# FoX scores with a full-height low pass, and mLSTM and sample FoX prepared one step ahead, in a hybrid decoder layer

## The chip, the cores and the metric

One Trainium2 chip, one of its cores. The metric is the device time of one execution in microseconds (us), lower is better. The kernel before takes 2261.63 us (median of 3 runs, 2254.97 to 2266.15).

## What is computed

One layer of a hybrid decoder for a prompt of 1024 tokens and a sample group of 8 sequences x 4 new tokens (32 rows), width 1024. One input projection `h @ w_in` feeds three mixers; their outputs are gated, merged and projected; cross attention and an MLP follow. All of it is float32. Of the mixers three matter here:

```python
# FoX: forgetting attention, 8 heads x 64, causal
s = einsum('bqhd,bkhd->bhqk', q, k) * hd**-0.5 + F_q - F_k      # F = cumsum(log sigmoid(f))
p = softmax(where(pos_q >= pos_k, s, -inf)); y = p @ v
# sample group: the same over 512 cached positions, gathered by page, and 4 new ones

# mLSTM: matrix memory, 4 heads x 128, chunk by chunk with a carried state C, n, m
d_w = exp(log_d - m_t); inter_w = exp(log_inter - m_t)
s   = (q @ k.T) * d_w
num = s @ v + inter_w * (C @ q); den = sum(s) + inter_w * (n . q)
h   = num / max(|den|, exp(-m_t))
C, n = a_end * C + (w_end * k).T @ v, a_end * n + (w_end * k) summed
y   = rmsnorm(h) * sigmoid(mo)
```

The prompt's mLSTM runs in 8 chunks of 128 tokens. The sample group's mLSTM is one chunk of 32 rows with 8 states that are loaded and written back.

## The kernel before

A float32 product is formed from float32r halves, in three passes: high x high, high x low, low x high (`mm3`, `split`). `load_u` and `load_tm` load 512 KB of weights from SP's queue (L61) into `wraw` (2 buffers); ScalarE writes the high half (`uh`, L54) and VectorE the low half (`ul`, L55). The products go into PSUM tiles called `mm`. The mixers use PSUM tiles `aux` (3) and `big` (1, two banks, for the scores).

The work is written as generators, and `weave` decides which of two takes the next step: the one that has got less far, by planned TensorE us (`k.pe`, counted from the matmuls' columns and from amounts added by hand) over a planned total. The line that matters:

```python
weave(k, (chain(pr["mq"], stage_gates(k)), 302.0), (mixers(), 312.0, 0.045, 0.95))
```

The main stream here is the projection of `mq` and of the gates, 28 weight units of 3 x 8 x 3 matmuls of 128 rows and 384 or 288 columns. The mixers run beside it from 4.5% to 95% of its way, in the order of `mixers()`: GLU, FoX of the prompt (`stage_fox`), mLSTM of the sample group (`stage_ml_sample`), then mLSTM of the prompt (`stage_ml`) together with FoX of the sample group (`stage_fox_sample`), woven by `beside` (so many steps of the first for one of the second), then the loading of two finished branches (`load_y`).

The order of writing is a priority, not yet the order on an engine: the framework's planner sorts each engine's instructions by a modelled time, taking the first in priority whose inputs are ready by its model. So gate matmuls stand between the four transposes of one mixer step in the trace. On the chip each engine and each DMA queue then follows this fixed order, and waits where the model was wrong.

Buffers: each stage has a pool of SBUF that is released at its end; the next stage's pool takes the same memory and must wait for the last reads of what lay there, DMA reads too. Within a pool a name has one to six buffers in turn.

`stage_fox` takes two heads at a time, at partitions 0 to 63 and 64 to 127. `KK[j]` has head j's keys as the high half on its own 64 partitions and the low half on the other 64. `QH[j]` has the query's high half on both, so one pass of 128 rows gives high x high and high x low. `QL` has the low halves of both heads, each on its own partitions; the second pass uses 64 rows of `QL` and of `KK[j]` (L229 is the helper that issues every matmul, L233 every transpose). A bf16 product with `identb` adds the causal mask. Widths go from 128 to 1024 columns, in pieces of up to 512, over 8 query blocks.

`ml_chunk` does one mLSTM chunk: it loads `km`, `v1`, `og` from POOL's queue (L1199), sets the ones column of `v1` on POOL (L1202), loads the row vector `E` broadcast to all partitions from SP's queue (L1204), adds the mask on VectorE (L1205) and takes the exponential on ScalarE (L1207); it transposes `km` into `kT`. Then come scores (`q,kT`), their product with `E` (L1217), `kw` (L1220), `num` from `v,E` and `CT,q`, the normalisation (L1231 to L1245), the state update (`v,kw`), and the tail: transposes of `yml` and the write to `S_yb`. `delayed_tails` takes the tail of one chunk after the second step of the next. Everything of a chunk is written in that chunk.

`stage_fox_sample` gathers pages of 128 positions x 512 values with indirect DMAs from POOL (L1067 keys, L1100 values) into `kt` (6 buffers), four for each of 16 steps, in the step that uses them. Its matmuls use one quarter of the array's columns per sequence (`tile_position`).

Of the kernel before, what the change touches and what calls it, by code (L numbers as in the profile page):

```python
# [18 lines left out]
P = 128  # L19
# [875 lines left out]
def stage_fox(k):  # L895
    nc, A, S = k.nc, k.A, k.S
    V, T, Sc = nc.vector, k.T, nc.scalar
    with ExitStack() as es:
        pool = es.enter_context(k.tc.tile_pool(name="fox", bufs=1, reuse_waits="tile"))
        for hp in range(4):  # L900
            cs = slice(hp * P, hp * P + P)

            KK = [pool.tile([P, NP], F32R, name="KK%d" % j) for j in range(2)]
            QH = [pool.tile([P, NP], F32R, name="QH%d" % j) for j in range(2)]
            QL = pool.tile([P, NP], F32R, name="QL")
            v = pool.tile([P, 8, P], F32, name="v", bufs=2)
# [10 lines left out]
            for i, tm in enumerate(tms):  # L917
                for h in range(2):
                    pt = k.aux.tile([P, 512], F32, name="aux")
                    for a in range(4):  # L920
                        T.transpose(pt[:, a * P:a * P + P], tm[:, 4 * h + a], k.ident)
                    c = slice(512 * h, 512 * h + 512)
                    for j in range(2):
                        r, o = half[j], half[1 - j]
                        hi = (KK, QH)[i][j]
                        Sc.activation(hi[r, c], pt[r], AF.Copy)
                        if i == 0:
                            V.tensor_tensor(hi[o, c], pt[r], hi[r, c].bitcast(F32), op=OP.subtract)
                        else:
                            Sc.activation(hi[o, c], pt[r], AF.Copy)  # L930
                            V.tensor_tensor(QL[r, c], pt[r], hi[r, c].bitcast(F32), op=OP.subtract)
                    k.pe += 1.5
                    yield
# [3 lines left out]
            def scores(u):  # L937
                qt, j = units[u]
                nk = (qt + 1) * P
                rows = slice(64 * j, 64 * j + 64)  # L940
                ps = k.big.tile([P, 1024], F32, name="big")
                for c0 in range(0, nk, 512):
                    n = min(512, nk - c0)
                    qc = slice(qt * P, qt * P + P)
                    T.matmul(ps[:, c0:c0 + n], QH[j][:, qc], KK[j][:, c0:c0 + n], start=True, stop=False)
                    T.matmul(ps[:, c0:c0 + n], QL[rows, qc], KK[j][rows, c0:c0 + n], start=False, stop=c0 + n < nk)
                T.matmul(ps[:, nk - P:nk], k.identb, k.maskq, start=False, stop=True)
                s = pool.tile([P, NP], F32, name="s", bufs=2)[:, :nk]
                mx = pool.tile([P, 1], F32, name="mx", bufs=2)
                V.tensor_tensor_reduce(s, ps[:, :nk], nF[j][:, :nk], 1.0, -3.0e38, OP.add, OP.max, mx)  # L950
                nm = pool.tile([P, 1], F32, name="nm", bufs=2)
                V.tensor_scalar(nm, mx, -1.0, None, op0=OP.mult)
# [79 lines left out]
def stage_fox_sample(k, pool):  # L1032
# [14 lines left out]
    for j in range(2):  # L1047
        r = slice(64 * j, 64 * j + 64)
        for b in range(4):
            dst = Qb[r, :, b].rearrange("p s (t h) -> p s t h", h=8)[:, :, :, 2 * b + j]  # L1050
            V.tensor_copy(dst, pq[r, b * NS:b * NS + NS].rearrange("p (s t) -> p s t", t=4))
    for g in range(2):
        pS = k.aux.tile([P, 512], F32, name="aux")
# [8 lines left out]
        for j in range(4):  # L1062
            kts = []
            for i in range(4):
                s = 4 * g + i
                kts.append(pool.tile([P, 512], F32, name="kt", bufs=6))
                nc.gpsimd.indirect_dma_start(  # L1067
                    out=kts[i], out_offset=None, in_=A["kp"],
                    in_offset=bass.IndirectOffsetOnAxis(ap=k.idx[:, 4 * s + j:4 * s + j + 1], axis=0))
# [25 lines left out]
        for j in range(4):  # L1095
            vts = []
            for i in range(4):
                s = 4 * g + i
                vts.append(pool.tile([P, 512], F32, name="kt", bufs=6))
                nc.gpsimd.indirect_dma_start(  # L1100
                    out=vts[i], out_offset=None, in_=A["vp"],
                    in_offset=bass.IndirectOffsetOnAxis(ap=k.idx[:, 4 * s + j:4 * s + j + 1], axis=0))
# [5 lines left out]
        Y = pool.tile([P, 512], F32, name="kt", bufs=6)  # L1108
        V.tensor_tensor(Y, pO, k.maskh, op=OP.mult)
# [78 lines left out]

def ml_chunk(k, pool, ti, n, qf, mask, inter, state):

    nc, S = k.nc, k.S
    V, T, Sc = nc.vector, k.T, nc.scalar
    t0 = TT[ti][0]
    km = pool.tile([P, 4, P], F32, name="km", bufs=2)[:n]
    v1 = pool.tile([P, 4, 129], F32, name="v1", bufs=2)[:n]
    og = pool.tile([P, 4, P], F32, name="og", bufs=2)[:n]
    for t, nme in ((km, "mk"), (v1, "mv"), (og, "og")):
        if ti < 8:
            nc.gpsimd.dma_start(t[:, :, 0:P], S[nme][t0:t0 + n, :].rearrange("p (a b) -> p a b", a=4))  # L1199
        else:  # L1200
            load_s(k, t, nme)
    nc.gpsimd.memset(v1[:, :, P:129], 1.0)  # L1202
    E = pool.tile([P, 4, P], F32, name="E", bufs=2)[:n, :, :n]
# [8 lines left out]
    Sc.activation(kT, pt[:, :4 * n], AF.Copy)  # L1212
# [5 lines left out]
    kw = pool.tile([P, 4, P], F32, name="kw", bufs=2)[:n]  # L1218
# [3 lines left out]
    num = pool.tile([P, 4, 129], F32, name="num", bufs=2)[:n]  # L1222
    for hh in range(2):
# [26 lines left out]
    for h in range(4):  # L1250
        T.transpose(py[:, h * n:h * n + n], y[:, h], k.ident[:n, :n])
    yf = pool.tile([P, 4 * P], F32, name="yf", bufs=2)[:, :4 * n]
# [5 lines left out]
def delayed_tails(gens, steps):  # L1258

    prev = None  # L1260
    for g in gens:
        n = 0
        for tag in g:
            yield
            n += 1
            if n == steps and prev is not None:
                yield from prev
                prev = None
            if tag == "tail":
                break  # L1270
        prev = g
    yield from prev


def stage_ml(k):
    nc, A, S = k.nc, k.A, k.S
    V, T, Sc = nc.vector, k.T, nc.scalar
    with ExitStack() as es:
        pool = es.enter_context(k.tc.tile_pool(name="ml", bufs=1, reuse_waits="tile"))
        CT = pool.tile([P, 4, 129], F32, name="CT")  # L1280

        def chunk(c):
            q4 = pool.tile([P, 4, P], F32, name="q4", bufs=2)
            nc.gpsimd.dma_start(q4, S["mqT"][:, :, c * P:c * P + P].rearrange("h p t -> p h t"))

            def inter(hh, pn, num):
# [24 lines left out]

            yield from ml_chunk(k, pool, c, P, lambda h: q4[:, h], k.maskt, inter, state)
        yield from delayed_tails((chunk(c) for c in range(8)), 2)
        nc.gpsimd.dma_start(k.O["mlCp"], CT)


def stage_ml_sample(k):
    nc, A, S = k.nc, k.A, k.S
    V, T, Sc = nc.vector, k.T, nc.scalar
    with ExitStack() as es:  # L1320
# [33 lines left out]

        yield from ml_chunk(k, pool, 8, NS, lambda h: qs[:, h], k.masks[:NS].rearrange("p (a b) -> p a b", a=4), inter, state)
        nc.gpsimd.dma_start(k.O["mlCs"], CS)
# [394 lines left out]
def build(es, tc, A, O, stop=None):  # L1751
# [268 lines left out]
```

## Time and profile before

| | us |
|---|---|
| median of the runs | 2261.63 (2254.97 to 2266.15) |
| the profiled execution | 2252.1 |
| its span, first to last instruction | 2250.3 |
| TensorE (PE) busy | 2181.9 |
| VectorE (DVE) busy | 1174.1 |
| ScalarE (ACT) busy | 677.2 |
| GpSimd (POOL) busy | 330.8 |

How to read it. PE is matmuls, PEld weight loads, which overlap them; matmul ends are modelled, so a busy PE is not PE at its peak, and start-to-start distances say more. SP is the engine that only issues DMAs. A group of instructions is named `out<-in`, with the array's rows and columns in use (`128*128`), the moving operand's shape, and how many. "Issue" is time in which an engine waited for nothing that the profile shows. The granted clock is the share of TensorE's full clock that was given. The FoX prompt attention runs from about 540 to 812 us, the sample mLSTM from 812 to 861, mLSTM with the sample's FoX from 861 to 1062; the gates' matmuls lie between them all the way. After 1160 come branches, cross attention and MLP, which the change does not touch.

### The profile page before, as it was taken

How to read it: one execution, taken by the hardware profiler on the slowest of the kernel's cores; microseconds unless marked ns; L12 is line 12 of the kernel's file. 1: busy time of each engine (PE TensorE's matmuls, PEld its weight loads, DVE VectorE, ACT ScalarE, POOL GpSimd, SP SyncE). 2: the span in 40 equal slices, each digit the busy share in tenths (PEclk: the TensorE clock that was granted, in tenths of full speed). 3: DMA queues.
4: the chain of work that ended last, by engine and by line, in shares of the span. 5: the costliest groups of instructions: out<-in, count | busy, mean ns of one | idle time of the engine just before them, and what ended most of it. 6: DMA issues, size and time to landing. Idle time of an engine off the chain costs nothing.

```text
span 2250.3 us, 39044 instructions
## 1 busy us (share of the span) xinstructions
PE 2181.9 (97%) x15926; PEld 2053.4 (91%) x15926; DVE 1174.1 (52%) x3103; ACT 677.2 (30%) x1350; POOL 330.8 (15%) x458
## 2 busy tenths in 40 slices
PE   6998999999999998999999999999999999999999
PEld 6998999998887887766999998999999999999999
DVE  5689966554667644543446445674333333333332
ACT  6433333323434422322312233542212122121220
POOL 1134100122000013444042113120000000000001
PEclk9999999999999998999999999999999999999999
DMA  8523433344322225665545312311111111111112
GB/s 286 172 70 114 153 100 113 114 171 141 91 76 77 69 85 160 200 186 177 217 155 174 132 47 75 96 38 47 48 47 40 46 48 47 48 47 47 48 38 77
DMA packets 104890, 231.81 MB, mean 103 GB/s; under 512 B 15724, under 2 KB 60860, under 8 KB 103936
## 3 DMA queue, kind: packets, MB, share of 16 engines
q0 software_dynamic: 28960, 102.82, 13.8%
q1 hardware_dynamic: 39480, 95.79, 13.4%
q10 hardware_dynamic: 36272, 30.72, 4.1%
q8 instruction: 125, 2.05, 0.4%
q14 instruction: 53, 0.43, 0.1%
HBM read 176.50 MB, written 52.78 MB: 102 GB/s over the span
## 4 chain that ended last, share of the span: by engine, by line
PE 78%; issue 7%; DVE 7%; DMA 4%; POOL 2%; ACT 1%; ACTq 0%; SPq 0%; POOLq 0%; DVEq 0%
PE mm L229 65%; PE aux L229 7%; PE big L229 3%; PE aux L233 3%; DMA wraw<-in_wt 1%; DMA E<-S_nM 1%; DVE ul L55 1%; DMA kt<-in_vp,idx 0%; DVE pe L448 0%; ACT uh L54 0%; DMA kt<-in_kp,idx 0%; DMA out_mlCs<-CS 0%; PE hold L229 0%; DVE pe L447 0%; DVE pss L436 0%
## 5 line engine op out<-in xcount | busy, mean ns | idle before, releaser
L229 PE MATMUL mm<-hch,uh 128*128 128x384 f32 (+1 forms) x1248 | 388.5, 324 | 0.0
L229 PE MATMUL mm<-hch,ul 128*128 128x384 f32 (+1 forms) x1152 | 371.2, 322 | 0.0
L229 PE MATMUL mm<-hcl,uh 128*128 128x384 f32 (+1 forms) x1056 | 339.9, 322 | 0.0
L54 ACT ACTIVATE uh<-wraw 128x1024 fp32r<-128x1024 f32 x156 | 165.0, 1058 | 579.8 <-PE mm L229 503.4
L229 PE MATMUL mm<-uh,hh 128*128 128x256 f32 x896 | 257.1, 287 | 10.6 <-ACT pq L435 10.1
L229 PE MATMUL mm<-ul,hh 128*128 128x256 f32 x896 | 253.3, 283 | 0.9 <-DVE ul L55 0.9
L229 PE MATMUL mm<-uh,hl 128*128 128x256 f32 x896 | 252.9, 282 | 0.0
L229 PE MATMUL mm<-fl,uh 128*128 128x384 f32 (+1 forms) x768 | 247.8, 323 | 0.0
L229 PE MATMUL mm<-fh,ul 128*128 128x384 f32 (+1 forms) x768 | 247.8, 323 | 0.0
L229 PE MATMUL mm<-fh,uh 128*128 128x384 f32 (+1 forms) x768 | 247.7, 323 | 0.0
L229 PEld LDWEIGHTS mm<-hch,uh 128*128 128x128 f32 x1248 | 231.9, 188 | 1.9 <-issue 1.6
L55 DVE TENSOR_TENSOR ul<-wraw,uh 128x1024 fp32r<-128x1024 f32 x156 | 193.9, 1243 | 63.9 <-ACT uh L54 63.9
L229 PE MATMUL mm<-hh,uh 128*128 128x384 f32 (+1 forms) x672 | 225.8, 336 | 0.0
L229 PE MATMUL mm<-hh,ul 128*128 128x384 f32 (+1 forms) x672 | 225.0, 335 | 0.0
L229 PE MATMUL mm<-hl,uh 128*128 128x384 f32 (+1 forms) x672 | 224.3, 334 | 0.0
L229 PEld LDWEIGHTS mm<-hch,ul 128*128 128x128 f32 x1152 | 217.1, 188 | 0.1
L1727 DVE TENSOR_TENSOR x<-x,mm 128x384 f32<-128x384 f32 (+1 forms) x192 | 99.8, 520 | 218.1 <-PE mm L229 218.1
L229 PEld LDWEIGHTS mm<-hcl,uh 128*128 128x128 f32 x1056 | 198.9, 188 | 0.0
L229 PEld LDWEIGHTS mm<-uh,hh 128*128 128x128 f32 x896 | 171.2, 191 | 14.0 <-ACT pq L435 10.5
L229 PEld LDWEIGHTS mm<-ul,hh 128*128 128x128 f32 x896 | 170.7, 191 | 1.5 <-DVE ul L55 1.1
L229 PEld LDWEIGHTS mm<-uh,hl 128*128 128x128 f32 x896 | 171.2, 191 | 0.0
L229 PEld LDWEIGHTS mm<-fl,uh 128*128 128x128 f32 x768 | 144.3, 188 | 0.0
(595 smaller groups left out, 3978.3 us busy)
## 6 DMA issues: line engine op xcount, KB each, us to landing
wraw<-in_wu SPq DMA_DIRECT2D x72, 512.0 KB, 3.6
wraw<-in_wd SPq DMA_DIRECT2D x50, 512.0 KB, 3.5
wraw<-in_wt SPq DMA_DIRECT2D x36, 512.0 KB, 5.5
gt<-S_gt POOLq DMA_DIRECT2D x24, 528.0 KB, 3.9
S_gt<-pf ACTq DMA_DIRECT2D x48, 192.0 KB, 1.9
bl<-S_yb POOLq DMA_DIRECT2D x3, 2112.0 KB, 12.1
x<-in_xT POOLq DMA_DIRECT2D x8, 528.0 KB, 5.2
nF<-S_nF POOLq DMA_DIRECT2D x8, 512.0 KB, 4.1
```

What stands on the lines that cost most here:

```text
L54: k.nc.scalar.activation(hi, src, AF.Copy)
L55: (eng or k.nc.vector).tensor_sub(lo, src, hi.bitcast(F32))
L229: return self.t.matmul(out, lhsT, rhs, **kw)
L233: return self.t.transpose(*a)
L1727: V.tensor_tensor(xs, xs, ps, op=OP.add)
```

## The change

1. `QL` becomes two tiles, `QL[0]` and `QL[1]`, allocated once and cleared once on the half that belongs to the other head; the second score pass uses all 128 rows of `QL[j]` and `KK[j]`. The products of the cleared rows are zero.
2. `ml_chunk` is cut in two. `ml_pre` does the loads, the mask, the exponential and the transposes of `km`. `stage_ml` calls it for chunk c + 1 before chunk c's own steps (`ahead`). `v1` is now two tiles that stay, with their ones columns set once on VectorE; `kw`, `num` and `yf` have one buffer in place of two. The tail of a chunk is taken after the third step of the next.
3. `stage_fox_sample` writes the gathers of a group one group before the use (`gather`, `take`), with nine `kt` buffers, and yields before the first group and between gathers and matmuls.
4. In `mixers()` the sample mLSTM stands before the prompt's FoX; its `ml_pre` adds 12 planned us and a step before the rest; `beside` gets 66 / 37 in place of 90 / 20.

```diff
@@ stage_fox
+        QL = [pool.tile([P, NP], F32R, name="QL%d" % j) for j in range(2)]
+        for j in range(2):
+            nc.gpsimd.memset(QL[j][64 * (1 - j):64 * (1 - j) + 64].bitcast(F32), 0.0)
         for hp in range(4):
...
-            QL = pool.tile([P, NP], F32R, name="QL")
...
-                            V.tensor_tensor(QL[r, c], pt[r], hi[r, c].bitcast(F32), op=OP.subtract)
+                            V.tensor_tensor(QL[j][r, c], pt[r], hi[r, c].bitcast(F32), op=OP.subtract)
...
-                    T.matmul(ps[:, c0:c0 + n], QL[rows, qc], KK[j][rows, c0:c0 + n], start=False, stop=c0 + n < nk)
+                    T.matmul(ps[:, c0:c0 + n], QL[j][:, qc], KK[j][:, c0:c0 + n], start=False, stop=c0 + n < nk)
@@ stage_fox_sample
+    order = [(g, src, j) for g in range(2) for src in ("kp", "vp") for j in range(4)]
+    ready = {}
+
+    def gather(n):
+
+        if n >= len(order):
+            return
+        g, src, j = order[n]
+        ts = ready[order[n]] = [pool.tile([P, 512], F32, name="kt", bufs=9) for _ in range(4)]
+        for i, t in enumerate(ts):
+            c = 4 * (4 * g + i) + j
+            nc.gpsimd.indirect_dma_start(out=t, out_offset=None, in_=A[src],
+                                         in_offset=bass.IndirectOffsetOnAxis(ap=k.idx[:, c:c + 1], axis=0))
+
+    def take(*key):
+        gather(order.index(key) + 1)
+        return ready.pop(key)
+
+    gather(0)
+    yield
...
-            kts = []
...
+            kts = take(g, "kp", j)
+            yield
...
-            vts = []
...
+            vts = take(g, "vp", j)
+            yield
@@ ml_chunk
-def ml_chunk(k, pool, ti, n, qf, mask, inter, state):
+def ml_pre(k, pool, ti, n, mask, v1):
...
-    v1 = pool.tile([P, 4, 129], F32, name="v1", bufs=2)[:n]
...
-    nc.gpsimd.memset(v1[:, :, P:129], 1.0)
...
-    yield
+    return km, og, E, kT
+
+
+def ml_chunk(k, pool, ti, n, pre, v1, qf, inter, state):
...
@@ stage_ml
+        def ahead(c):
             q4 = pool.tile([P, 4, P], F32, name="q4", bufs=2)
             nc.gpsimd.dma_start(q4, S["mqT"][:, :, c * P:c * P + P].rearrange("h p t -> p h t"))
+            return q4, ml_pre(k, pool, c, P, k.maskt, v1s[c % 2])
...
-        yield from delayed_tails((chunk(c) for c in range(8)), 2)
+        nxt, prev = ahead(0), None
+        yield
+        for c in range(8):
+            g = chunk(c, *nxt)
+            nxt = ahead(c + 1) if c < 7 else None
+            yield
+            n = 0
+            for tag in g:
+                yield
+                n += 1
+                if n == 3 and prev is not None:
+                    yield from prev
+                if tag == "tail":
+                    break
+            prev = g
+        yield from prev
@@ stage_ml_sample
+        v1 = pool.tile([NS, 4, 129], F32, name="v1")
+        V.memset(v1[:, :, P:129], 1.0)
+        pre = ml_pre(k, pool, 8, NS, k.masks[:NS].rearrange("p (a b) -> p a b", a=4), v1)
+        k.pe += 12.0
+        yield
+        yield from ml_chunk(k, pool, 8, NS, pre, v1, lambda h: qs[:, h], inter, state)
@@ mixers
         yield from stage_glu(k)
+        yield from stage_ml_sample(k)
         yield from stage_fox(k)
-        yield from stage_ml_sample(k)
         with tc.tile_pool(name="foxs", bufs=1, reuse_waits="tile") as fp:
-            yield from beside(stage_ml(k), stage_fox_sample(k, fp), 90 / 20)
+            yield from beside(stage_ml(k), stage_fox_sample(k, fp), 66 / 37)
```

More of the change, by code (lines that the diff above doesn't have):

```diff
@@ L939, in scores @@
                 nk = (qt + 1) * P
-                rows = slice(64 * j, 64 * j + 64)
                 ps = k.big.tile([P, 1024], F32, name="big")
@@ L1062, in stage_fox_sample @@
         for j in range(4):
-            kts = []
[L1064 to L1069, printed above, removed]
+            kts = take(g, "kp", j)
+            yield
             for b in range(4):
@@ L1095, in stage_fox_sample @@
         for j in range(4):
-            vts = []
[L1097 to L1102, printed above, removed]
+            vts = take(g, "vp", j)
+            yield
             for i, o in enumerate(rows):
@@ L1107, in stage_fox_sample @@
             T.matmul(pO[o, :], pTn[:, o], tms["fv"], start=False, stop=True, tile_position=(0, 32 * i))
-        Y = pool.tile([P, 512], F32, name="kt", bufs=6)
+        Y = pool.tile([P, 512], F32, name="kt", bufs=9)
         V.tensor_tensor(Y, pO, k.maskh, op=OP.mult)
@@ L1186, in stage_ml_rows @@
         yield
-def ml_chunk(k, pool, ti, n, qf, mask, inter, state):
+def ml_pre(k, pool, ti, n, mask, v1):
     nc, S = k.nc, k.S
-    V, T, Sc = nc.vector, k.T, nc.scalar
+    T, Sc = k.T, nc.scalar
     t0 = TT[ti][0]
     km = pool.tile([P, 4, P], F32, name="km", bufs=2)[:n]
-    v1 = pool.tile([P, 4, 129], F32, name="v1", bufs=2)[:n]
     og = pool.tile([P, 4, P], F32, name="og", bufs=2)[:n]
@@ L1212, in ml_chunk @@
     Sc.activation(kT, pt[:, :4 * n], AF.Copy)
-    yield
+    return km, og, E, kT
+def ml_chunk(k, pool, ti, n, pre, v1, qf, inter, state):
+    nc, S = k.nc, k.S
+    V, T, Sc = nc.vector, k.T, nc.scalar
+    t0 = TT[ti][0]
+    km, og, E, kT = pre
     ps = k.aux.tile([P, 512], F32, name="aux")
@@ L1217, in ml_chunk @@
     V.tensor_tensor(E, E, ps[:n, :4 * n].rearrange("p (a b) -> p a b", a=4), op=OP.mult)
-    kw = pool.tile([P, 4, P], F32, name="kw", bufs=2)[:n]
+    kw = pool.tile([P, 4, P], F32, name="kw", bufs=1)[:n]
     for h in range(4):
@@ L1221, in ml_chunk @@
     yield
-    num = pool.tile([P, 4, 129], F32, name="num", bufs=2)[:n]
+    num = pool.tile([P, 4, 129], F32, name="num", bufs=1)[:n]
     for hh in range(2):
@@ L1251, in ml_chunk @@
         T.transpose(py[:, h * n:h * n + n], y[:, h], k.ident[:n, :n])
-    yf = pool.tile([P, 4 * P], F32, name="yf", bufs=2)[:, :4 * n]
+    yf = pool.tile([P, 4 * P], F32, name="yf", bufs=1)[:, :4 * n]
     Sc.activation(yf, py[:, :4 * n], AF.Copy)
@@ L1255, in ml_chunk @@
     yield
[L1258 to L1272, printed above, removed]
 def stage_ml(k):
@@ L1280, in stage_ml, with chunk @@
         CT = pool.tile([P, 4, 129], F32, name="CT")
-        def chunk(c):
+        v1s = [pool.tile([P, 4, 129], F32, name="v1%d" % i) for i in range(2)]
+        for v1 in v1s:
+            V.memset(v1[:, :, P:129], 1.0)
+        def ahead(c):
             q4 = pool.tile([P, 4, P], F32, name="q4", bufs=2)
             nc.gpsimd.dma_start(q4, S["mqT"][:, :, c * P:c * P + P].rearrange("h p t -> p h t"))
+            return q4, ml_pre(k, pool, c, P, k.maskt, v1s[c % 2])
+        def chunk(c, q4, pre):
             def inter(hh, pn, num):
@@ L1310, in state @@
                             V.scalar_tensor_tensor(CT[:, h], CT[:, h], k.aend[:, h, c:c + 1], src, op0=OP.mult, op1=OP.add)
-            yield from ml_chunk(k, pool, c, P, lambda h: q4[:, h], k.maskt, inter, state)
-        yield from delayed_tails((chunk(c) for c in range(8)), 2)
+            yield from ml_chunk(k, pool, c, P, pre, v1s[c % 2], lambda h: q4[:, h], inter, state)
+        nxt, prev = ahead(0), None
[14 more added lines that the diff above has]
+        yield from prev
         nc.gpsimd.dma_start(k.O["mlCp"], CT)
@@ L1353, in state @@
                                                pc[:, (h % 2) * 129:(h % 2) * 129 + 129], op0=OP.mult, op1=OP.add)
-        yield from ml_chunk(k, pool, 8, NS, lambda h: qs[:, h], k.masks[:NS].rearrange("p (a b) -> p a b", a=4), inter, state)
+        v1 = pool.tile([NS, 4, 129], F32, name="v1")
+        V.memset(v1[:, :, P:129], 1.0)
+        pre = ml_pre(k, pool, 8, NS, k.masks[:NS].rearrange("p (a b) -> p a b", a=4), v1)
+        k.pe += 12.0
+        yield
+        yield from ml_chunk(k, pool, 8, NS, pre, v1, lambda h: qs[:, h], inter, state)
         nc.gpsimd.dma_start(k.O["mlCs"], CS)
```

## The prediction

> **What bounds the kernel now.** I read the page first: engine busy times, then the waits, then stages.
>
> ```profile
> span 2250.3 us, 39044 instructions
> PE 2181.9 (97%) x15926; PEld 2053.4 (91%) x15926; DVE 1174.1 (52%) x3103; ACT 677.2 (30%) x1350; POOL 330.8 (15%) x458
> ```
>
> TensorE is busy for 97% and idle for 68 us. So an edit pays only if it shortens TensorE's own stream or removes its idle time. The stages that the change touches, by windows (length, busy time of PE, PEld, DVE, ACT, POOL, granted clock, DMA share, GB/s): FoX prompt attention, mLSTM of the sample group, mLSTM prompt with sample FoX, and what follows.
>
> ```profile
> 540.00:812.00 272.00, 270.70 (x1885) 217.35 (x1886) 181.74 (x481) 110.69 (x240) 13.19 (x19) 1.00 0.27 84
> 812.00:861.00 49.00, 49.00 (x326) 43.35 (x323) 22.96 (x88) 8.41 (x20) 4.37 (x9) 1.00 0.16 53
> 861.00:1062.00 201.00, 178.16 (x1203) 133.03 (x1203) 83.81 (x323) 52.62 (x122) 91.48 (x113) 0.93 0.65 193
> 1062.00:1160.00 98.00, 98.00 (x615) 98.00 (x615) 44.23 (x58) 27.88 (x36) 19.61 (x25) 1.00 0.53 191
> ```
>
> In the first window TensorE never rests, so what is left to win there lies inside its busy time. The third is the only one with much idle time, and the only one with a clock below 1. Its TensorE waits (total us, times, longest):
>
> ```profile
> PE aux L233 <- DVE yml L1245: 6.6, 3, 3.4
> PE aux L229 <- issue: 6.0, 1, 6.0
> PE aux L229 <- ACT kT L1212: 3.6, 1, 3.6
> PE aux L229 <- DMA kt<-in_kp,idx: 2.8, 5, 1.1
> PE aux L229 <- DMA kt<-in_vp,idx: 2.3, 3, 1.0
> PE aux L229 <- DVE num L1298: 1.4, 1, 1.4
> ```
>
> **Edit 1: the low pass on all 128 rows.** One FoX score tile in the timeline (start, duration), then a narrower one:
>
> ```profile
> 800.75 0.49 PE L229 MATMUL big<-KK,QH 128*128 128x512 f32 x1
> 801.18 0.49 PE L229 MATMUL big<-KK,QL 64*128 64x512 f32 x1
> 801.60 0.23 PE L229 MATMUL big<-maskqb,identb 128*128 128x128 bf16 x1
> ...
> 707.60 0.38 PE L229 MATMUL big<-KK,QH 128*128 128x256 f32 x1
> 707.91 0.38 PE L229 MATMUL big<-KK,QL 64*128 64x256 f32 x1
> ```
>
> From start to start a 512-wide pass takes 0.42 to 0.43 us and a 256-wide one 0.31. Uniform runs of 128-row matmuls of the same type go faster, in the chain of waits (start, length): 96 of width 256, and 24 of width 384.
>
> ```profile
> 250.97 11.42 PE mm L229 x96
> ...
> 675.47 4.22 PE mm L229 x24
> ```
>
> That is 0.119 and 0.176 us each, so 0.057 per 128 columns and 0.233 for 512. Every pass next to a 64-row one thus costs about 0.19 us more than its columns, at both widths: this extra follows the change between 64 and 128 rows, not the work. Making QL full height keeps the columns (a matmul's time goes by columns in these rows) and removes the changes. All passes together, in the FoX window:
>
> ```profile
> 540.00:812.00 272.00, 72.20 (x189) 34.93 (x189) 8.09 (x12) 7.02 (x12) 1.00 0.27 84
> ```
>
> Now 72.2 us (the rows that read KK, 189 recorded of 192). Less the last pass's tail beyond the mask's start (801.18 + 0.49 - 801.60 = 0.07, in 64 score tiles, 4.5): 68. After: each pair of heads has 2 heads x 128 x (1+...+8) columns in two passes, 18,432; four pairs 73,728, or 576 x 0.057 = 33, and 0.005 for each of 192 instructions (0.119 - 2 x 0.057): 34. **Gain 34 us**, bounds 28 (128-wide passes that go no faster than 256-wide ones, and some extra left at the tile's ends) to 38 (0.2 x 192). The copies and subtractions stay the same. The two new clears are not in the trace; the nearest row clears as many columns:
>
> ```profile
> 873.29 0.97 POOL L1041 MEMSET Qb<- 128x1024 f32 x1
> ```
>
> So 2 us, on an engine that is busy 13 of 272 us there. DVE, with 182 of 272 us, would have 182 of 238: still no bound.
>
> [...]
>
> **Edit 2: mLSTM chunks prepared a chunk ahead, and the sample mLSTM moved ahead of FoX.** The start of the stage now:
>
> ```profile
> 861.12 0.59 POOL L1356 DMA_DIRECT2D out_mlCs<-CS  x1 [43.92 <-DVE CS L1352]
> ```
> ```profile
> 857.54 19.57 SPq L61 DMA_DIRECT2D wraw<-in_wu  x2
> 877.20 14.10 SPq L1204 DMA_DIRECT2D E<-S_nM  x3
> ```
> ```profile
> 876.00:908.00 32.00, 23.12 (x133) 17.60 (x134) 11.54 (x47) 7.14 (x20) 8.63 (x11) 0.63 0.49 141
> 908.00:1062.00 154.00, 140.80 (x984) 101.54 (x982) 70.59 (x273) 42.80 (x98) 74.08 (x89) 0.99 0.68 198
> ```
>
> The state's write-out (861.12) holds the memory that the next pools take; the first E waits on SP's queue behind weight loads to 877.2. TensorE idles 3.6 + 6.0 us (the waits on kT and on "issue" above: first score and value matmuls), and after it the clock is 0.63 for 32 us: 23.1 x 0.37 = 8.6 us lost. Together 18. Afterwards the write-out no longer stands before this stage, but its tiles must still wait for FoX's last reads, and the plan's idea of how long a load takes stays as it is. **I take half, 9**; bounds 0 and 18.
>
> Within the stage the waits are 6.6 + 1.4 + 2.8 + 2.3 = 13.1, and 1% of 140.8 in clock: 14.5. The longest comes through VectorE's in-order queue: the mask add of the next E waits for its load, and behind it stands the normalisation that TensorE needs:
>
> ```profile
> 940.71 0.69 DVE L1205 TENSOR_TENSOR E<-E,masktb 128x512 f32<-128x512 f32 x1 [3.85 <-DMA E<-S_nM]
> ...
> 946.52 1.14 DVE L1245 SCALAR_TENSOR_TENSOR yml<-num,d,og 128x128 f32<-128x128 f32 x4
> ```
>
> A chunk's lead and gathers one group early should hide most: **9 saved**, bounds -48 (rival 3) and 14.5. Tails one step later and the single kw, num and yf cost nothing: a whole chunk, 201 / 8 = 25 us with what is woven in, lies between two uses. The ones columns set once save POOL a clear a chunk, off the path.
>
> **Edit 3: gathers one group ahead, nine buffers for six.** The matmuls on gathered tiles use a quarter of the array's columns each. When the four operands come one by one, they run alone; when all are there, side by side:
>
> ```profile
> 1052.59 1.04 PE L229 MATMUL aux<-kt,pT 128*32 128x512 f32 x2
> 1053.57 0.44 PE L229 MATMUL mm<-hh,ul 128*128 128x384 f32 x1
> ...
> 1059.37 1.06 PE L229 MATMUL aux<-tfv,pTn 32*32 32x512 f32 x8
> ```
> ```profile
> L229 PE MATMUL aux<-kt,pT 128*32 128x512 f32 x64 | 23.7, 604 | 2.3 <-DMA kt<-in_vp,idx 2.3
> L229 PE MATMUL aux<-kt,Qb 128*32 128x128 f32 x256 | 16.6, 281 | 2.8 <-DMA kt<-in_kp,idx 2.8
> ```
> ```profile
> 1006.33 1.10 PE L229 MATMUL aux<-kt,Qb 128*32 128x128 f32 x32
> ```
>
> Two alone take 0.98 us, eight side by side 1.06. With whole groups the first kind needs 8 x 1.06 = 8.5 for 23.7, the second 8 x 1.1 = 8.8 for 16.6: 23 us at most, inside "busy" time. A gather's issue takes 0.94 us and lands in 4.1 (below), so a group of four is there in 8, about one step's distance: **12 saved**, bounds 0 and 23.
>
> ```profile
> L1100 POOL DMA_INDIRECT kt<-in_vp,idx x32: 940/946/1831, 928.7 to 1051.7; - x32
> DMA to landing us min/median/max: 3.2/4.1/8.9
> ```
>
> **What is late next.** The write-out now stands before FoX, on POOL's queue ahead of the clears (QL may take its memory) and of FoX's tm, v and nF loads; KK cannot be written before it ends:
>
> ```profile
> out_mlCs<-CS POOLq DMA_DIRECT2D x1, 2064.0 KB, 8.6
> tm<-S_fk POOLq DMA_DIRECT2D x4, 512.0 KB, 5.2
> ```
>
> 8.6 + 2 + 5.2 = 16 us until scores can start, against gate matmuls that the plan can pull in front, as it did at 817 to 861. **I take 4 lost**; bounds 0 and 18 (the price of the same write-out above). At its new start the sample stage waits for GLU's weights to be released, then for CS, 2 MB as in the write-out, so about 8.6; the 12 us of gate work now counted in between cover it (uncovered: 8.6). The mixers' planned cost grows by 12 to some 316 of 312, so they end at 0.045 + 0.905 x 316 / 312 = 96% of the gates; the remaining 11 us of gate work and the two branch loads' own steps cover the last splits: nothing.
>
> **Sum**, against the profiled execution's 2252.1 us (1.8 around the span): -34 - 9 - 9 - 12 + 4 = -60, so 2192. The runs' median, 2261.6, lies 9.5 above that execution; I add half of it, 5, for a median: **2197**.
>
> **Rivals.** (1) Only the low pass pays; the stalls move to the new order's seams, since the plan's load times are unchanged. 2252 - 34 + 4 + 5 = 2227. For it: 18 of 33 us of stalls came at a seam, and seams remain. Against: the write-out leaves this one. (2) The low pass gains nothing, the rest does: 2252 - 26 + 5 = 2231. [...] (3) The early mask adds block VectorE in every chunk. E loads land in 6.8 us (median; first to last 4.5 to 8.1):
>
> ```profile
> DMA to landing us min/median/max: 4.5/6.8/8.1
> DVE E L1205 <- DMA E<-S_nM: 19.8, 6, 6.2
> ```
>
> An add that is placed ahead of the running chunk's chain and waits for a whole load costs TensorE up to 6.8; eight are 54 for today's 6.6: 2252 - 34 + 48 + 5 = 2271 with nothing else won, slower. It decides from 34 + 6.6 = 40.6 us, six of eight loads uncovered. Against: VectorE waited 19.8 us for E already, and a third of it reached TensorE. (4) Gains and new stalls cancel (QL 28, the seam 18, other waits 10 more): 2257. (5) All bounds come out well: 2252 - 38 - 18 - 14 - 23 + 5 = 2164.
>
> **Chances.** Forecast 0.48 (its own range 2176 to 2218), (1) 0.27, (2) 0.05, (3) 0.07, (4) 0.06, (5) 0.07. This kernel's measurement tells 0.5% (11 us) from no change. Faster: forecast, (1), (2), (5), 0.87; same 0.06; slower 0.07. The range 2170 to 2238 holds forecast, (1) and (2), about eight in ten.
>
> **What would show it.** Edit 1: QL rows as 128*128, 512-wide passes 0.23 us apart, KK's busy time near 38. Edit 2: no wait on E or kT in TensorE's list, clock 1 throughout. Edit 3: kt,pT near 9 us, in groups of eight. The seam: idle time and a dip of the clock where FoX begins. The forecast is wrong if the passes stay 0.4 us apart, or if this idle time exceeds 10 us.

## The result and the profile after

The changed kernel takes 2202.51 us (median of 4 runs, 2197.55 to 2209.93), the kernel before 2259.89 in the same comparison: ratio 0.9747, 95% interval 0.9709 to 0.9786. Five later runs beside the last experiments gave 2206.1 us and a ratio of 0.9782 (0.9763 to 0.9801). The second ratio is the better guide: the four runs of the kernel before in the first comparison have a median 6 us above the medians of the 37 later ones (2253.2 to 2254.1). Forecast were 2197 and a gain of 60 us on the profiled execution; that execution went from 2252.1 to 2204.5, a gain of 47.6, which fits the ratio of 0.9782 (49 us).

The page of the changed kernel begins with the span and TensorE's (PE's) busy time:

```profile
span 2202.8 us, 39045 instructions
PE 2139.2 (97%) x15926; PEld 2050.5 (93%) x15926; DVE 1174.4 (53%) x3106; ACT 677.2 (31%) x1350; POOL 332.8 (15%) x451
```

Busy time fell by 42.7 us, the rest of the span (span less busy time, called idle below) from 68.4 to 63.6. So by this count, of one profile each, nearly all of the gain is shorter busy time on TensorE, and next to nothing is removed waiting. The experiments show below that the count misleads about one edit. The windows of its stages (same columns as in the prediction): FoX, now behind the sample mLSTM; mLSTM with the sample's FoX; what follows.

```profile
570.00:830.00 260.00, 257.04 (x1927) 226.43 (x1927) 186.61 (x498) 116.27 (x250) 19.40 (x26) 0.99 0.32 103
830.00:1016.00 186.00, 167.93 (x1289) 138.47 (x1287) 89.03 (x332) 53.37 (x126) 88.95 (x102) 0.93 0.68 199
1016.00:1160.00 144.00, 144.00 (x901) 143.98 (x901) 62.94 (x86) 31.70 (x39) 36.29 (x46) 1.00 0.50 174
```

The mLSTM stage is 15 us shorter, but still idles for 18 us, and its clock is 0.93 as before. To compare kernels whose stages lie a little differently, I use one window, 800 to 1080 us, which holds this stage in all of them. The kernel before, then the changed one:

```profile
800.00:1080.00 280.00, 256.13 (x1740) 203.25 (x1740) 122.88 (x434) 72.81 (x158) 101.48 (x131) 0.95 0.58 177
```
```profile
800.00:1080.00 280.00, 261.87 (x1915) 228.66 (x1912) 138.46 (x424) 86.14 (x177) 95.25 (x113) 0.95 0.61 188
```

Idle 23.9 against 18.1 us; clock 0.95 in both, which is 13 us of busy time at a clock of 1 lost in each. TensorE's waits in the changed kernel are many and short (five rows of its list of waits: total us, count, longest), and of those shown one small one is put down to a load:

```profile
PE aux L233 <- ACT yf L1271: 3.1, 1, 3.1
PE aux L229 <- DVE E L1235: 3.0, 2, 1.8
PE aux L233 <- DVE CT L1318: 2.7, 1, 2.7
PE aux L229 <- ACT bt L1304: 2.6, 1, 2.6
PE aux L229 <- DMA kt<-in_vp,idx: 0.8, 1, 0.8
```

A score tile in the changed kernel's timeline, and the row of all passes (those that read KK) by windows:

```profile
816.31 0.50 PE L229 MATMUL big<-KK,QH 128*128 128x512 f32 x1
816.64 0.40 PE L229 MATMUL big<-KK,QL 128*128 128x512 f32 x1
816.88 0.34 PE L229 MATMUL big<-KK,QH 128*128 128x384 f32 x1
817.05 0.34 PE L229 MATMUL big<-KK,QL 128*128 128x384 f32 x1
817.23 0.23 PE L229 MATMUL big<-maskqb,identb 128*128 128x128 bf16 x1
```
```profile
530.00:830.00 300.00, 50.46 (x192) 32.62 (x192) 10.85 (x16) 9.27 (x16) 0.99 0.32 102
```

Inside the tile a 512-wide pass now takes 0.24 us and a 384-wide one 0.17 to 0.18. This tile's first pass keeps some extra (0.33); in other tiles it does not (at 814.08 us of the same trace it takes 0.23). From each pass to the start of the next matmul, all 192 take 38.3 us, where they took 66.6. The matmuls on gathered tiles, by lines:

```profile
L229 PE MATMUL aux<-kt,Qb 128*32 128x128 f32 x256 | 13.7, 291 | 0.0
L229 PE MATMUL aux<-kt,pT 128*32 128x512 f32 x64 | 10.6, 604 | 0.8 <-DMA kt<-in_vp,idx 0.8
```

Together 24.3 us, where it was 40.3. And the new seam ahead of FoX, on POOL and by windows:

```profile
576.38 0.59 POOL L1386 DMA_DIRECT2D out_mlCs<-CS  x1 [36.98 <-DVE CS L1377]
583.27 1.95 POOL L903 MEMSET QL<- 64x1024 f32 x2 [6.30 <-DMA out_mlCs<-CS]
585.18 0.90 POOL L914 DMA_DIRECT2D tm<-S_fk  x1
```
```profile
560.00:580.00 20.00, 20.00 (x116) 17.67 (x115) 12.97 (x46) 2.64 (x5) 0.59 (x1) 0.91 0.28 97
580.00:600.00 20.00, 18.69 (x122) 17.86 (x122) 7.29 (x12) 8.14 (x16) 8.27 (x10) 1.00 0.86 287
```

The clears wait 6.3 us for the write-out, as foretold, and TensorE feels 1.3 us of idle time (0.3 in the second profile of the same kernel). The clock of 0.91 in the first window does not come from that wait. From 576.1 to 578.7 us gate matmuls of 384 columns start every 0.32 us, where they took 0.175 before. That begins while TensorE is busy, just before the write-out is issued at 576.38.

### The profile page after: what moved, and what is told of

Its sections match the earlier page's. It is cut to its first block, busy times and chain, and to the rows that moved or that the text cites. A ratio compares the mean times of both kernels' runs of the same rounds, so it can differ in the third digit from the quotient of the medians.

```text
span 2202.8 us, 39045 instructions
## 1 busy us (share of the span) xinstructions
PE 2139.2 (97%) x15926; PEld 2050.5 (93%) x15926; DVE 1174.4 (53%) x3106; ACT 677.2 (31%) x1350; POOL 332.8 (15%) x451
## 4 chain that ended last, share of the span: by engine, by line
PE 52%; DVE 2%; DMA 0%; ACT 0%; issue 0%; ACTq 0%
PE mm L229 49%; PE aux L229 2%; PE aux L233 0%; PE hold L229 0%; DVE hcl L120 0%; DVE ul L55 0%; DMA kt<-in_vp,idx 0%; DVE x L1495 0%; ACT uh L54 0%; DVE rmt L111 0%; DVE rmr L113 0%; DVE rxt L112 0%; DVE rmt L112 0%; DVE dg L145 0%; DVE rxt L111 0%
## 5 line engine op out<-in xcount | busy, mean ns | idle before, releaser
L55 DVE TENSOR_TENSOR ul<-wraw,uh 128x1024 fp32r<-128x1024 f32 x156 | 193.8, 1243 | 62.6 <-ACT uh L54 59.9
```

The source lines that it names most:

```text
L55: (eng or k.nc.vector).tensor_sub(lo, src, hi.bitcast(F32))
```

## The experiments

All kernels side by side. Ratio is to the kernel before, from runs on the same chip; the columns behind it come from each kernel's own profile, one execution each (idle is span less busy time; the stage's idle time and clock are those of the window 800 to 1080; kt is kt,pT plus kt,Qb).

| kernel | ratio (95%) | span | busy | idle | stage idle | stage clock | kt |
|---|---|---|---|---|---|---|---|
| before | 1 | 2250.3 | 2181.9 | 68.4 | 23.9 | 0.95 | 40.3 |
| changed | 0.9747 (0.9709-0.9786) | 2202.8 | 2139.2 | 63.6 | 18.1 | 0.95 | 24.3 |
| before + low pass | 0.9907 (0.9882-0.9932) | 2227.6 | 2155.2 | 72.4 | 26.4 | 0.95 | 40.3 |
| before + gathers | 1.0014 (0.9998-1.0031) | 2248.3 | 2176.1 | 72.2 | 29.1 | 0.95 | 36.3 |
| before + chunk lead | 0.9942 (0.9920-0.9963) | 2234.5 | 2170.6 | 63.9 | 19.0 | 0.98 | 35.3 |
| before, passes grouped | 0.9956 (0.9937-0.9976) | 2251.3 | 2175.7 | 75.6 | 29.1 | 0.92 | 41.7 |
| changed, order back | 0.9817 (0.9787-0.9848) | 2213.5 | 2148.2 | 65.3 | 19.5 | 0.91 | 28.8 |
| changed, no early gathers | 0.9774 (0.9754-0.9794) | 2201.9 | 2142.8 | 59.1 | 12.7 | 0.98 | 33.9 |
| changed, 64-row low pass | 0.9931 (0.9908-0.9954) | 2240.3 | 2170.4 | 69.9 | 18.6 | 0.94 | 23.3 |
| changed, E x 3 | 0.9780 (0.9755-0.9805) | 2199.2 | 2138.0 | 61.2 | 14.4 | 0.96 | 23.6 |
| changed, again | 0.9782 (0.9763-0.9801) | 2204.4 | 2140.6 | 63.8 | 17.6 | 0.95 | 23.9 |
| changed, more gate work | 0.9776 (0.9755-0.9797) | 2206.0 | 2140.8 | 65.2 | 20.4 | 0.94 | 23.7 |
| the same, no early gathers | 0.9757 (0.9738-0.9776) | 2196.6 | 2137.1 | 59.5 | 15.9 | 0.96 | 29.3 |
| more gate work, split write-out | 0.9780 (0.9752-0.9807) | 2190.4 | 2127.8 | 62.6 | 17.1 | 0.98 | 22.1 |

The first four make single edits to the kernel before. In the code, `...` and comments stand for longer parts.

**The low pass alone.**

```diff
-            QL = pool.tile([P, NP], F32R, name="QL")            # in the loop over pairs of heads
+        QL = [pool.tile([P, NP], F32R, name="QL%d" % j) for j in range(2)]   # ahead of it, cleared once
-                    T.matmul(ps[:, c0:c0 + n], QL[rows, qc], KK[j][rows, c0:c0 + n], ...)
+                    T.matmul(ps[:, c0:c0 + n], QL[j][:, qc], KK[j][:, c0:c0 + n], ...)
```

> The kernel before with edit 1 alone (full-height low pass). My theory: the score passes' start-to-start time falls from 67 to 38 us as in the changed kernel and all of it reaches the end, because TensorE has no idle time there: 28 us less, ratio 0.987 to 0.988, TensorE's idle time within 3 us of before. Rival: VectorE and the single score buffer set FoX's pace, so that the saved time comes back as idle time or is lost in the stage behind: under 12 us less, ratio above 0.994.

Busy time fell by 26.7 us, close to the 28 expected; the time by 0.93%, 21 us, between theory and rival. The missing part is idle time: 4 us more over the span. It is not in FoX, whose rows show no new wait of weight. The wait that stands out lies at the start of the mLSTM stage, one of 10.5 us:

```profile
PE aux L229 <- issue: 15.2, 3, 10.5
PE aux L233 <- DVE yml L1247: 4.8, 3, 3.2
```

In the kernel before, the longest such wait is 6.0. So edit 1 is worth 27 us on TensorE, and in this kernel some of it comes back as waiting at the next seam.

**The gathers alone**, with single kw, num and yf so that nine buffers fit.

```diff
-        # gathers written in the step that uses them, kt bufs=6
+        # gather(n + 1) written one group ahead, kt bufs=9 (as in the change)
-            yield from beside(stage_ml(k), stage_fox_sample(k, fp), 90 / 20)
+            yield from beside(stage_ml(k), stage_fox_sample(k, fp), 90 / 37)
```

> The kernel before with edit 3 alone: gathers a group ahead, nine buffers (room made by single kw, num and yf as in the change), step ratio 90/37 for the new number of steps. Theory: whole groups are what lets the quarter-array matmuls run side by side, so kt,pT falls from 24 us to about 12 and the time by 10 to 14 us, ratio 0.994 to 0.996. Rival: the grouping comes from the new chunk order and step ratio, not from the early gathers: kt,pT stays above 18 us and the time within 5 us of before.

The theory fell. No gain (1.0014), and the groups formed only in part, 20.2 for 23.7 us, while the wait for yml grew from 6.6:

```profile
L229 PE MATMUL aux<-kt,pT 128*32 128x512 f32 x64 | 20.2, 603 | 2.4 <-DMA kt<-in_vp,idx 2.4
```
```profile
PE aux L233 <- DVE yml L1255: 11.0, 4, 3.9
```

**The chunk lead alone.**

```diff
-    # ml_chunk loads, masks and transposes its own chunk; tails after step 2
+    # ml_pre for chunk c + 1 ahead of chunk c, two lasting v1 tiles, tails after step 3 (as in the change)
-            yield from beside(stage_ml(k), stage_fox_sample(k, fp), 90 / 20)
+            yield from beside(stage_ml(k), stage_fox_sample(k, fp), 66 / 20)
```

> The kernel before with the chunk lead, persistent value tiles and late tails alone; sample mLSTM still behind FoX, gathers as before, step ratio 66/20. Theory: the lead by itself does little, since the planner already issued each E load as soon as its buffer was free: within 6 us of before (ratio 0.997 to 1.002), stage idle time 15 to 23 us, VectorE still waits about 12 to 20 us for E loads. Rival (the prediction's own step): stalls inside the stage fall by 9 us or more, ratio 0.996 or less.

Here the rival holds as to the time: 0.58% less, 13 us. Over the whole span the profiled run had the highest clock of the five (0.994, the others 0.988 to 0.991; the kernel before 0.987 to 0.992), so the clock's part of the gain is smaller in the others. In the profiled run the stage's idle time fell by 5 us and its clock rose to 0.98, which is 5.2 us lost for 12.8:

```profile
800.00:1080.00 280.00, 261.04 (x1842) 216.14 (x1841) 134.12 (x451) 80.77 (x169) 103.83 (x122) 0.98 0.59 185
```

It did so although VectorE still waited 16.2 us for E loads (19.8 before). Two waits are no longer in TensorE's list: the one for yml behind such a load, 6.6 us, and the one of 6.0 us at the stage's start. In return the waits for gathered keys grew from 2.8 to 6.8 us. Most of the gain lies at the start:

```profile
876.00:908.00 32.00, 25.18 (x211) 19.93 (x210) 14.77 (x57) 9.83 (x24) 18.19 (x20) 0.93 0.70 213
```

In the kernel before, this window has 23.12 us of busy time and a clock of 0.63. Idle time and lost clock from 861 to 908 us fall from 18.2 to 8.6, from 908 to 1062 only from 14.6 to 12.5. The write-out still stands in front of the stage, issued at 862.19 us. But the first E load is issued at 862.00, where it stood behind weight loads until 877.20.

**The passes in another order**, to see what the extra 0.19 us is paid for.

```diff
-                for c0 in range(0, nk, 512):      # high pass, low pass, per piece of 512 columns
-                    T.matmul(... QH ...); T.matmul(... QL ...)
+                for c0 in range(0, nk, 512): T.matmul(... QH ...)
+                for c0 in range(0, nk, 512): T.matmul(... QL ...)
```

> The kernel before with only the order of the score passes changed: in a score tile wider than 512 both high passes, then both 64-row low passes, so two changes of height per tile in place of four, with the same passes. If the extra 0.19 us is paid at each change of height: 32 wide tiles x 2 x 0.19 = 12 us less, ratio 0.994 to 0.996. If a 64-row pass and the pass behind it each pay: one fewer extra per tile, 6 us less. If 64-row passes are slow in themselves: the second low pass keeps its 0.42 us and the time stays within 3 us.

The timeline, where two equal passes in a row are one row:

```profile
790.55 0.73 PE L229 MATMUL big<-KK,QH 128*128 128x512 f32 x2
791.21 0.73 PE L229 MATMUL big<-KK,QL 64*128 64x512 f32 x2
791.87 0.23 PE L229 MATMUL big<-maskqb,identb 128*128 128x128 bf16 x1
```
```profile
530.00:830.00 300.00, 61.62 (x192) 31.79 (x192) 10.77 (x16) 9.27 (x16) 1.00 0.29 94
```

Four passes take 1.32 us from first start to mask, where four alternating ones took 4 x 0.425 = 1.70. The difference is 2 x 0.19, for two changes of height fewer. Two 64-row passes in a row take 0.66, which is one plain 0.233 and one 0.43: a 64-row pass behind another is not slow. All passes together fell from 73.1 to 61.6 us in this window, 11.5 of the 12 expected. So the extra is paid at each change of height. The time fell by 0.44% (10 us, interval 5 to 14), which alone would not tell 12 from 6; the timeline does. The profiled execution is the slowest of the ten runs, and its span shows nothing of the gain.

The next four take single parts out of the changed kernel or add to it.

**The order put back.**

```diff
-        yield from stage_ml_sample(k)
         yield from stage_fox(k)
+        yield from stage_ml_sample(k)
```

> The changed kernel with the sample mLSTM put back behind the prompt's FoX; everything else of the change stays. Theory: the write-out of the sample states then again holds the memory of the mLSTM stage, TensorE idles 9 us more at its start and loses 8 us to a low clock: 10 to 18 us slower than the changed kernel, ratio to the kernel before 0.979 to 0.983. Rival: the stall only moves with the write-out to FoX's start, so the order makes no difference: within 4 us of the changed kernel (ratio 0.973 to 0.977).

2212.4 us, 6 to 10 more than the two medians of the changed kernel, and 10 more than two kernels on the same chip that take the changed kernel's time (no early gathers, E x 3). That is the first theory's time, at its lower end, but not its mechanism. The stage's idle time grew by 1.4 us, not by 9; it is the clock that fell:

```profile
800.00:1080.00 280.00, 260.53 (x1774) 224.31 (x1773) 125.98 (x420) 75.79 (x159) 93.42 (x111) 0.91 0.58 178
```

260.5 x 0.09 = 23 us of clock lost, more than the 19.5 us of idle time in the same window. A third of it lies where TensorE never waits, and most of that before the write-out is issued at 843.29 us:

```profile
828.00:846.00 18.00, 18.00 (x70) 16.32 (x69) 6.91 (x19) 0.80 (x2) 2.25 (x4) 0.53 0.25 88
```

So the order is worth some us, but that the write-out is the reason is not shown.

**No early gathers in the changed kernel.**

```diff
-            kts = take(g, "kp", j)       # gathered one group ahead, kt bufs=9, 66 / 37
+            # four gathers here, kt bufs=6, 66 / 20 (as in the kernel before); vts alike
```

> The changed kernel without edit 3: gathers written in the step that uses them, six buffers, step ratio 66/20; everything else of the change stays. Theory after the runs of the single edits: early gathers do nothing alone but make whole groups once the chunks are prepared ahead: kt,pT goes back from 10.6 to about 18 us, and the time is 8 to 14 us longer than the changed kernel (ratio to before 0.979 to 0.981). Rival: the chunk lead and the order carry the whole gain behind FoX: within 4 us of the changed kernel.

The rival holds: 2202.6 us, the same time. Its rows show where edit 3's gain goes:

```profile
L229 PE MATMUL aux<-kt,pT 128*32 128x512 f32 x64 | 18.6, 630 | 1.6 <-DMA kt<-in_vp,idx 1.4
L229 PE MATMUL aux<-kt,Qb 128*32 128x128 f32 x256 | 15.3, 287 | 4.5 <-DMA kt<-in_kp,idx 4.0 <-issue 0.4
```
```profile
800.00:1080.00 280.00, 267.31 (x1952) 227.92 (x1951) 143.11 (x433) 89.27 (x184) 96.24 (x113) 0.98 0.61 189
```

With early gathers these matmuls are 9.6 us shorter (24.3 for 33.9), but idle time in the stage is 5.4 us longer (18.1 for 12.7) and the clock loses 13.1 us (261.9 x 0.05) in place of 5.3 (267.3 x 0.02). The runs bear out the clock: over the whole span it is 0.991 to 0.992 in three of the four runs without early gathers (the fourth shows 0.942 without a longer time, which is not explained), and 0.986 to 0.991 in the nine of the changed kernel.

**The 64-row low pass in the changed kernel.**

```diff
-                    T.matmul(ps[:, c0:c0 + n], QL[j][:, qc], KK[j][:, c0:c0 + n], ...)
+                    T.matmul(ps[:, c0:c0 + n], QL[64 * j:64 * j + 64, qc], KK[j][64 * j:64 * j + 64, c0:c0 + n], ...)
```

> The changed kernel with the 64-row low pass put back; the rest of the change stays. Theory: the 28 us that the passes save reach the end in full here, since no write-out stands before the next stage to hand any back: ratio to before 0.985 to 0.989, 25 to 31 us slower than the changed kernel. Rival: as in the kernel with this edit alone, some 6 to 8 us of it are lost in the stage behind, so putting it back costs 20 us or less (ratio 0.982 to 0.984).

2241.2 us, 35 to 39 more. That is above both ranges. On the profiles TensorE's busy time is 31.2 us longer, 4.5 more than the low pass alone changed it. Its idle time is 6.3 us longer, as much as one wait at FoX's start, on the write of KK:

```profile
PE aux L233 <- DVE KK L929: 6.4, 1, 6.4
```

In these two kernels the waits at a seam thus moved by several us in opposite directions: here they add to edit 1's worth, in the kernel with the low pass alone they took from it.

**Three buffers for E.**

```diff
-    E = pool.tile([P, 4, P], F32, name="E", bufs=2)[:n, :, :n]
+    E = pool.tile([P, 4, P], F32, name="E", bufs=3)[:n, :, :n]      # and yml bufs=1 for the room
```

> The changed kernel with three buffers for E in place of two (room from a single yml), so that each E load can be issued one chunk earlier still; nothing else. Theory: the stage's remaining idle time (18 us) hangs on the late E loads, for which VectorE still waits 11.5 us: those waits go below 3 us, idle time in the stage falls by 6 us or more, and the time by 5 to 10 us (ratio to before 0.970 to 0.973). Rival: other short chains (bt, yf, CT, q) take their place: VectorE's waits for E go, the idle time stays within 4 us, and so does the time.

VectorE's waits for E loads fell only from 11.5 to 7.5 us, the stage's idle time by 3.7, and the time not measurably (0.9780). TensorE's waits for the product of the scores with E (L1235) grew from 3.0 to 7.2 us. That is the rival: other chains take their place.

The last four ran beside each other on one chip, five runs each.

> The changed kernel, unchanged, beside the next three on the same chip, for a closer interval: ratio to before 0.973 to 0.979. It leaves 18 us of idle time and 12 us of lost clock in the mLSTM stage; the runs so far say that edit 3 shortens the matmuls there by 9 us and that idle time and clock give the same 9 us back.

0.9782, as expected.

**More gate work beside the mLSTM stage.**

```diff
-            yield from beside(stage_ml(k), stage_fox_sample(k, fp), 66 / 37)
+            for v in beside(stage_ml(k), stage_fox_sample(k, fp), 66 / 37):
+                k.pe += 0.25
+                yield v
-    weave(k, (chain(pr["mq"], stage_gates(k)), 302.0), (mixers(), 312.0, 0.045, 0.95))
+    weave(k, (chain(pr["mq"], stage_gates(k)), 302.0), (mixers(), 338.0, 0.045, 0.95))
```

> The changed kernel with more gate matmuls woven into the mLSTM stage and fewer into FoX and GLU: 0.25 planned us more for each step of that stage, and 338 in place of 312 as the mixers' planned total, so that the stage gets about 16 us more of gate work. Theory: the stage waits because its chunks' serial chains have too little other work beside them, and this is where edit 3's gain went: idle time and lost clock of the stage fall from 30 us to under 18, the time by 8 to 14 us (ratio to before 0.969 to 0.972). Rival: the waits come from loads that land later than the plan has it, whatever stands beside them: idle time and clock within 5 us of the changed kernel, same time; or FoX, with less gate work, now waits instead.

The theory fell: same time (0.9776), 20.4 us of idle time and a clock of 0.94. The edit did bring the work: from the stage's first score product to its last transpose of yml the gates' matmuls take 84.7 us, where they take 70.6 in the changed kernel. So a lack of other work is not what holds the stage.

> As the run with more gate work in the mLSTM stage, but without edit 3 (gathers in their own step, six buffers, 66/20). Theory: with enough work beside the chains the early gathers are worth their 9 us of matmul time, so this is 6 to 12 us slower than the same kernel with them. Rival: early gathers are worth nothing here either, since what they free is waited away: within 4 us.

0.9757 without the early gathers, against 0.9776 with them. The intervals overlap, as each holds the spread of the kernel before; the runs themselves hardly do. The five without early gathers take 2197.5 to 2201.3 us. All five of the changed kernel (2203.0 to 2206.9) are longer, and four of the five with the same added gate work (2200.5 to 2208.3) are too. So neither expectation holds: here the early gathers cost about 5 us, with 5.6 us less in matmuls, 4.5 us more idle time and a lower clock over the span (0.987 to 0.989 for 0.991 to 0.993). The lowest median of all kernels, 2199.3, is one without edit 3.

**The write-out one sequence at a time**, with the added gate work.

```diff
+                nc.gpsimd.dma_start(k.O["mlCs"][:, s], CS[:, s])      # in the loop over sequences
-        nc.gpsimd.dma_start(k.O["mlCs"], CS)
```

> As the run with more gate work in the mLSTM stage, and the sample states are written out one sequence at a time (eight writes of 258 KB, each behind its own update) in place of one write of 2 MB at the stage's end. Theory: FoX's start then waits for one eighth of the write-out; the wait of 6.3 us for it before the clears of QL, the dip of the clock to 0.91 there and 2 to 5 us of time go. Rival: FoX's start is held by its own loads, and the time stays within 2 us.

The clears wait 2.5 us in place of 6.3 and come at 574.1 in place of 583.8 us (the run with more gate work and one write); at FoX's start the clock stays at 1:

```profile
574.08 1.95 POOL L903 MEMSET QL<- 64x1024 f32 x2 [2.48 <-DMA out_mlCs<-CS]
```
```profile
560.00:600.00 40.00, 38.03 (x243) 33.29 (x243) 24.61 (x73) 15.70 (x35) 11.67 (x16) 1.00 0.62 202
```

The kernel with one write also has a clock of 1.00 and less idle time in the same 40 us (0.6 for 2.0 us), so nothing is won at that place. The profiled span with split writes, 2190.4, is the shortest of all, but that is its run with the highest clock (0.994, the others 0.986 to 0.991). Its runs go from 2192.7 to 2210.5 and its ratio is that of the changed kernel: no gain that can be told from none.

## Why the prediction was right, point by point

The time, the sign and the likeliest case hold: 2202.5 lies 5.5 above the forecast. But the terms of the sum did not come in as written, and their errors partly cancel.

*Edit 1, 34 us (28 to 38).* The mechanism is right and shown twice: the extra belongs to the change of height (grouped passes), and it goes when QL has full height. Its size is 28.3 us from start to start (66.6 to 38.3), 26.7 in busy time with the low pass alone, so at the lower bound. The term was mis-sized at the step "at the pace of uniform runs". Between passes that pace came, but 43 of the 78 passes that come first behind another kind of matmul keep about 0.1 us each. All that remains above the pace, at the last passes too, is 4.7 us. The 68 before were also 1.4 too many. The sign that KK's busy time would be near 38 was set wrongly: it is 50.5, since modelled ends run past the next start by more than the 0.07 taken (817.05 + 0.34 is 0.16 past the mask's start). Distances from start to start were the measure to name; they give 38.

*Rival 2* (the low pass gains nothing) is out: two 128-row passes keep 0.24 us each at 512 columns.

*Edit 2, 9 at the start and 9 within.* The size came, in other places than written. The lead alone gave 13 us, and in its profile 9.6 of the idle time and lost clock that went lie at the stage's start, 2.1 behind it. It gave them with the write-out still in front. So by these two profiles about half of the loss at the start hung on what the prediction named beside the write-out, the first E load behind the weight loads. Within the stage the lead saved 2 us, not 9. The order gave 6 to 10 (order put back), but idle time at the write-out, the reason written for it, accounts for little of that. The signs set for edit 2 did not come either: in the changed kernel TensorE waits 3.0 us for the product with E, and the stage's clock is 0.93, not 1.

*Edit 3, 12 us.* This step failed. Its matmul side came in better than written, 16 us (24.3 for 40.3; some of it goes to the lead, which alone gives 35.3). Its step from matmul time to time did not: the prediction took what lies inside busy time as path. Taken out of the changed kernel, or put alone into the one before, the edit moves the time by nothing that can be measured; with more gate work it costs about 5 us. What it frees in matmuls returns as idle time and as lost clock. Why is not settled. Too little other work is ruled out by the run with more gate work, and E loads alone by the run with three buffers. The waits change place: with early gathers TensorE waits 3.1 us for yf, 3.0 for the product with E and 0.8 for gathered tiles, without them 0.7, none in the list, and 5.4. What remains are such short waits on chains of VectorE and ScalarE (yf, CT, E, bt), whose places in the engines' fixed orders the planner sets anew in every kernel; no run isolated them.

*The seam, 4 lost.* Measured 1.3 us of idle time, with the write-out, clears and loads in the order that was named. The dip of the clock that was set as its sign is there too, but stands before the wait.

*Sum.* 60 were forecast, 47.6 came. Edit 1 brought 27 of its 34 and edit 3 nothing measurable of its 12. Edit 2 and the seam together then brought 21, where 18 - 4 = 14 were written; that surplus hides a part of the two misses. The 5 us added for a median hide another: the profiled execution of the changed kernel lies 2 us above its median, not 5 below. That the forecast of the median is only 5.5 off is luck to that extent.

*Rival 1* (only the low pass pays) is out by the kernel with the low pass alone, 0.9907 for 0.9747 or 0.9782. *Rival 3* (mask adds block VectorE): VectorE's waits for E loads fell to 11.5 us, and no wait of TensorE in the stage is longer than 3.1 us, where an E load took 4.5 at the least in the kernel before. Rivals 4 and 5 are out by their times, 2257 and 2164.

## What to carry to other kernels

Where matmuls of different heights alternate, look at start-to-start distances: a zeroed half that keeps the array's full height cost TensorE nothing in these rows (its clears took 2 us of GpSimd, once), and removed 0.19 us at each change. Where a stage waits on many short chains, time saved in its matmuls is no saving until an experiment with that part alone says so; take a term that lies in such a stage at zero in the sum and keep its size for the range. Count the clock beside idle time: in the changed kernel's mLSTM stage they are 13 and 18 us. And read a difference in clock from several runs, since one profile shows one of them.

## What the runs showed of the hardware that was not expected

The clock fell after a shorter wait than in the kernel before, and in these traces a wait's length alone does not tell whether it falls. Before, it was low after waits of 3.4, 3.6 and 6.0 us. In the changed kernel it fell after one of 1.84 us:

```profile
852.73 1.14 PE L229 MATMUL aux<-v,E 128*128 128x129 f32 x4 [1.84 <-DVE E L1235]
```
```profile
848.00:852.00 4.00, 2.72 (x18) 2.12 (x17) 0.48 (x2) 0.30 (x1) 2.14 (x2) 1.00 0.89 288
852.00:856.00 4.00, 3.27 (x9) 1.76 (x9) 1.96 (x10) 1.38 (x4) 1.37 (x2) 0.60 0.78 272
856.00:860.00 4.00, 4.00 (x41) 2.79 (x41) 0.32 (x3) 0.00 (x0) 0.00 (x0) 0.50 0.08 29
```

In the kernel before, a wait of 2.73 us left the clock at 1:

```profile
1000.57 0.30 PE L233 MATMUL aux<-ctile,yml 128*128 128x128 f32 x1 [2.73 <-DVE yml L1245]
```
```profile
996.00:1000.00 4.00, 1.83 (x11) 1.56 (x9) 3.76 (x21) 1.81 (x5) 0.00 (x0) 1.00 0.03 9
1000.00:1004.00 4.00, 3.44 (x27) 3.26 (x28) 2.06 (x7) 1.73 (x5) 0.82 (x2) 1.00 0.39 123
```

In the traces of these two kernels each record of the granted clock is 1 or 0.5, so the 0.60 above is a mean. One wait comes in both: 1.82 us before the same product (`hsr,Cdr`), ending at 457.2 us in the kernel before and at 455.3 in the changed one. In the changed kernel the clock is at half for 3.41 us from 456.85 us on; in the kernel before it stays at 1. Two windows of that length of the first, then two of the second:

```profile
452.53:455.94 3.41, 2.84 (x17) 2.51 (x15) 3.10 (x18) 0.48 (x1) 0.15 (x1) 1.00 0.37 154
455.94:459.35 3.41, 2.17 (x25) 1.87 (x26) 2.23 (x12) 0.58 (x2) 0.99 (x3) 1.00 0.10 38
```
```profile
453.40:456.82 3.42, 1.60 (x22) 1.27 (x22) 2.77 (x15) 0.00 (x0) 0.87 (x2) 1.00 0.09 38
456.82:460.23 3.41, 3.41 (x12) 3.41 (x12) 1.76 (x3) 2.12 (x3) 2.14 (x5) 0.50 0.23 78
```

Before, the wait lies across both windows, TensorE is busy for 2.84 and 2.17 us of them, and the clock is 1 in both. In the changed kernel it lies in one window, with 1.60 us busy, and the clock of the next is 0.50. The wait of 2.73 us above lies for the most part in a window of 4 us with 1.83 us busy, and the clock of the next is 1. It also fell without a wait: ahead of FoX in the changed kernel TensorE is busy for all of the 3.41 us from 572.90 to 576.31, in 2.23 of them with products on 32 of the array's rows (`v,kwm` of the sample mLSTM), and the 3.42 us behind them have a clock of 0.50. What decides is not shown, and each clock in the table above is that of one run. Runs of one kernel differ in their clock too: of twenty of the kernel before, the five at a clock of 0.992 took 2245.7 to 2251.6 us, the three at 0.987 took 2257.7 to 2262.5. After the change, about two fifths of the stage's losses are lost clock (13 of 31 us).
